# Six more Strassen-like groups in a one-core decoder layer, and a second place for the sums of w_up's activations

## The chip, the core and the metric

The kernel runs on one core of one Trainium2 chip, in float32. The metric is the device time of one execution in microseconds (us); before the change three runs took 1473.76, 1474.32 and 1475.28 us, a median of 1474.32. The profile is of one execution, whose span (first to last instruction) is 1471.1 us.

TensorE (PE) multiplies, with PEld as its weight load; VectorE (DVE) does elementwise work; ScalarE (ACT) does activations and copies; GpSimd (POOL) does next to nothing here; SyncE (SP) issues the DMA of the weights.

## The reference

One decoder layer on 256 tokens with a width of 2048:

```python
u = rmsnorm(h, norm_mix_pre)
P = u @ w_in                               # SSD z, x, B, C, dt and attention q, k, v
y_mix = concat(ssd(P), attention(P))       # 256 x 4096
h = h + rmsnorm(y_mix @ w_out, norm_mix_post)
u = rmsnorm(h, norm_mlp_pre)
hdn = relu(u @ w_up)                       # 256 x 8192
h = h + rmsnorm((hdn * hdn) @ w_down, norm_mlp_post)
```

What the change touches are the products with `w_out` (4096 x 2048), `w_up` (2048 x 8192) and `w_down` (8192 x 2048).

## The kernel before

**Three products for one.** Every float32 operand is split in a high part (`hi`, a rounded copy by ScalarE, L139) and a low part (`lo`, the rest, a subtraction by VectorE, L140). A product is then three matmuls: high by high, high by low and low by high (L262 to L264, or L344 to L346). A weight tile `raw` of 2 x 128 rows and 512 columns is loaded by SyncE (L149), split, and its parts stand in `hi` and `lo`, with five buffers each (`BUFS`, L44). `raw` has four buffers, and two more in the place of `uc` while the activations of the first stage are not needed (`fetch_next`, L190).

**Ordinary groups and sevens.** A unit (`unit`, L362) computes 1024 columns of the output, two blocks of 512, for all 256 tokens (two tiles of 128). It goes through groups `k` of 256 rows. An ordinary group makes 2 x 2 x 2 block products, 8, that is 24 matmuls, from two weight tiles. A seven (`seven`, L311) makes the same with 7 block products, 21 matmuls, in the manner of Strassen and Winograd: it needs sums of the weight blocks (four additions of 512 columns on VectorE, into `e`, into `t4` and in place into `raw_b`, L320 to L325) and four split tiles in place of two (`hl_a`, `hl_e` and `hl_b` of 1024 columns, `hl_t` of 512). It also needs sums of the activation blocks (`sums_of_acts`, L293), which are made once for each `k` and kept in the memory that `room["sums"]` lists, two entries for each `k`. Four more accumulators in PSUM (`more`) are folded into the result after the last seven of a unit (`combine_new`, L348; `combine_onto`, L893).

**Which group is a seven** is written by hand at each unit: `order_of(ks, by_seven)` gives the order of the groups and the set of sevens, and then follow the closing sets, which are always ordinary and go block by block: both tokens of the first 512 columns, then of the second.

**What sets the order of the work.** The Tile framework schedules instructions by priority. Loading, adding and splitting weights have a high priority (`AHEAD`), and are chained in the order in which the code writes them (`line`, `in_line`, L209 to L225): a group's additions and splits come before the next group's on VectorE and ScalarE. The sums of the activations of the next group, if it is a seven, are asked for before the present group (L369).

**The stages.** w_out's first five groups (L1080) run while the last attention heads finish, whose products stand between the matmuls; then the attention's memory is closed and the pool `hp` opened in its place (L1085 to L1087), which holds `e`, the temporaries `r`, the residual `h` and the mixing result `mw`. w_out's first unit goes on with groups 5 to 13 and the closing sets 14 and 15 (L1118). Its second unit (L1144) ends in `mix_to_up` (L916), an order written out by hand, which finishes the mixing result, adds it to `h` and starts `w_up`; it uses the memory of `ua`, in which sums of the second unit stand, for four weight parts. Then `h` goes out to DRAM (`out_of_place`, L1194), and its memory serves the sums of the `w_up` units: `ha` has six entries, which is three sums (`UP_SEVENS`, L52, is groups 2, 4 and 5). The first half of `w_up` has three units (L1240, `fb` 2, 4 and 6), each with groups 0 to 5 and the closing sets 6 and 7; `up_end` and `turned` (L1205, L1216) square, turn and split the result. The two units of the first half of `w_down` (L1245, L1247), the four of the second half of `w_up` and the two of the second half of `w_down` (L1265, L1270) follow. In the second unit of the latter, group 9 is a seven already; in w_out's second unit groups 8 and 10 are.

Of the kernel before, what the change touches and what calls it, by code (L numbers as in the profile page):

```python
# [10 lines left out]
F32 = mybir.dt.float32  # L11
F32R = mybir.dt.float32r
# [4 lines left out]
P = 128  # L17
S = 256
D = 2048
NT = S // P  # L20
# [19 lines left out]
KB = 2  # L40
# [11 lines left out]
UP_SEVENS = (2, 4, 5)  # L52
# [22 lines left out]
def hymba_layer(ctx: ExitStack, tc: tile.TileContext, x, norm_mix_pre, w_in, conv_w, conv_b, dt_bias, a_log,  # L75
# [3 lines left out]
    w_in, w_out, w_up, w_down = w_in[0], w_out[0], w_up[0], w_down[0]  # L79
# [44 lines left out]
    def bank():  # L124
        return pacc.tile([P, NB], F32, name="acc")

    def psmall():
        return psm.tile([P, NB], F32, name="ps")
# [7 lines left out]
    def split(hi, lo, src, scale=None):  # L136

        if scale is None:
            return (nc.scalar.activation(hi, src, AF.Copy),  # L139
                    nc.vector.tensor_tensor(lo, src, hi.bitcast(F32), op=ALU.subtract))  # L140
        return (nc.scalar.activation(hi, src, AF.Copy, scale=scale),  # L141
                nc.vector.scalar_tensor_tensor(lo, src, scale, hi.bitcast(F32), op0=ALU.mult, op1=ALU.subtract))
# [10 lines left out]
    def tmp():  # L153
        if "own" in room:
            room["own"].rotate(1)
            return room["own"][0]
        return hp.tile([P, NB], F32, name="r", bufs=2)
# [6 lines left out]
    room = {}  # L164
# [6 lines left out]
        room["acts"] = part  # L171
        sums_of.clear()

    def in_place_of_h(acts):

        a = hp.tile([P, 3 * KB, 2, S], F32R, name="ha")
        room["sums"] = [a[:, k] for k in range(3 * KB)]
        if acts is part:
            b = hp.tile([P, KB, 2, S], F32R, name="hb")
            room["sums"] += [b[:, k] for k in range(KB)]  # L180
            room["sums"] += [hp.tile([P, 2, S], F32R, name="wpost", bufs=2) for _ in range(2)]
        else:
            b = hp.tile([P, NT, NB], F32, name="hb")
            room["shared"] = [[b[:, t] for t in range(NT)],
                              [hp.tile([P, NB], F32, name="wpost", bufs=2) for _ in range(NT)]]
        room["raw"] = None
        room["acts"] = acts
        sums_of.clear()
# [22 lines left out]
    @contextmanager  # L211
    def in_line():

        with ExitStack() as order:
            for last in line.values():
                order.enter_context(tc.issue_after(last.ins))
            yield

    def split_in_line(hi, lo, raw):
        with in_line():  # L220
            line["act"], line["dve"] = split(hi, lo, raw)

    def add_in_line(dst, a, b):
        with in_line():
            line["dve"] = nc.vector.tensor_tensor(dst, a, b, op=ALU.add)  # L225
# [26 lines left out]
    def drain():  # L252
        while waiting:
            pump()
# [11 lines left out]
    def row_tiles(src, c0, ks, acc, acts, first=True, last=True, lag=0, at_end=None, pumps=1, fetch=fetch):  # L266


        held = {}
        n = len(ks)  # L270
        for i in range(n + lag):
            if i < n:
                held[i] = weights(src, ks[i] * KB, c0, fetch)
            for t, at in ((0, i), (1, i - lag)):
                if not 0 <= at < n:
                    continue
                row_tile(acc[t], t, held[at], ks[at], acts, first and at == 0, last and at == n - 1)
                if at == n - 1 and at_end:
                    at_end(t, acc[t])
            pump(pumps)  # L280
# [12 lines left out]
    def sums_of_acts(k):  # L293

        if k in sums_of:
            return sums_of[k]
        places = room["sums"][2 * len(sums_of):][:2]
        h_, l_, r = room["acts"](k * KB)
        with tc.high_priority(offset=AHEAD):
            a, c = (tmp().rearrange("p (i s) -> p i s", s=P) for _ in range(2))  # L300
            ah_, al_ = (v[:, r:r + KB].bitcast(F32).rearrange("p j (t s) -> p j t s", t=NT) for v in (h_, l_))
            nc.vector.tensor_tensor(a.rearrange("p (j t) s -> p j t s", t=NT), ah_, al_, op=ALU.add)
            nc.vector.tensor_tensor(c[:, 0:2], a[:, 0::3], a[:, 1:2].to_broadcast([P, 2, P]), op=ALU.subtract)
            nc.vector.tensor_tensor(c[:, 2], a[:, 0], c[:, 1], op=ALU.add)
            nc.vector.tensor_tensor(c[:, 3], a[:, 2], c[:, 2], op=ALU.subtract)
            ch, cl = (v.rearrange("p b (t s) -> p (b t) s", t=NT) for v in places)
            split(ch, cl, c)
        sums_of[k] = ch, cl
        return ch, cl
# [38 lines left out]
    def combine_new(dst, more):  # L348

        with tc.high_priority(offset=AHEAD):  # L350
            a, b = dst
            u = tmp()
            nc.scalar.activation(a[0], more[0], AF.Copy)
            nc.vector.tensor_tensor(u, a[0], more[2], op=ALU.subtract)
            nc.vector.tensor_tensor(a[1], more[3], u, op=ALU.add)
            nc.vector.tensor_tensor(b[0], more[1], u, op=ALU.add)
            nc.vector.tensor_tensor(b[1], more[3], b[0], op=ALU.add)

    def order_of(ks, by_seven):
        return [(k, k in by_seven) for k in ks]  # L360

    def unit(src, n, order, last, acc, more, combine, lag=0, at_end=(None, None), first=True, ending=None):  # L362


        cols = (n * NB, (n + 1) * NB)
        sevens = [k for k, by_seven in order if by_seven]
        for i, (k, by_seven) in enumerate(order):
            if i + 1 < len(order) and order[i + 1][1]:
                sums_of_acts(order[i + 1][0])  # L369
            if by_seven:  # L370
                if k == sevens[0]:
                    drain()
                seven(src, *cols, k, acc, more, k == sevens[0], k == sevens[-1])
            else:
                for b in range(2):
                    row_tiles(src, cols[b], [k], acc[b::2], room["acts"], first and i == 0, False,
                              fetch=fetch_next)
            if k == sevens[-1]:
                combine(more)
        for b in range(2):  # L380
            if b and ending:
                ended.append(ending(cols[b], last, acc))
            else:
                row_tiles(src, cols[b], last, acc[b::2], room["acts"], False, True, lag if b else 0, at_end[b],
                          fetch=fetch if b else fetch_next)
# [692 lines left out]
    acc = [bank() for _ in range(2 * NT)]  # L1078
    early = 5
# [7 lines left out]
    hp = ctx.enter_context(tc.tile_pool(name="hp", bufs=1, reuse_waits="tile"))  # L1087
# [11 lines left out]
    mw = hp.tile([P, NT, D], F32, name="mw")  # L1099
# [10 lines left out]
    more = [psmall(), bank(), psmall(), bank()]  # L1110

    def whole(n):
        def at_end(t, a):
# [1 line left out]
                mixed(n, t, a)  # L1115
        return at_end

    unit(w_out, 0, order_of(range(early, 14), (6, 9, 12)), (14, 15), acc, more,  # L1118
         lambda x: combine_new(in_mw(0), x), 0, (whole(0), whole(1)), first=False)
    for n in (2, 3):  # L1120
        load_wpost(norm_mix_post, n)
    acc, more = more, acc
# [71 lines left out]
    def out_of_place():  # L1194

        yield from copies(in_dram, of_h, 4)
        in_place_of_h(act_u)
        for k in UP_SEVENS:
            sums_of_acts(k)
            yield  # L1200

    def in_dram(t, cs):
        return h_d[:, t, cs]
# [24 lines left out]
    acc = gemm_features(w_up, NB, begun)  # L1228
# [6 lines left out]
    acc, more = [bank() for _ in range(2 * NT)], [psmall(), bank(), psmall(), bank()]  # L1235
    for hf in range(2):
        if hf:
            in_place_of_h(act_u)
        for fb in range(0 if hf else 2, 8, 2):
            unit(w_up[:, hf * 4096:], fb, order_of(range(6), UP_SEVENS), (6, 7), acc, more,  # L1240
                 lambda x: combine_new(room["shared"], x), 0, (up_end(fb, 0), up_end(fb + 1, 1)))
            acc, more = more, acc
        if hf == 0:
            in_place_of_h(part)
            unit(w_down, 0, order_of(range(14), (4, 6, 9, 11, 13)), (14, 15), acc, more,  # L1245
                 lambda x: combine_new(in_mw(0), x), 0, (onto(0), onto(1)))
            unit(w_down, 2, order_of((0, 1, 4, 2, 6, 3, 9, 5, 11, 7, 13, 8), (4, 6, 9, 11, 13)), (10, 12, 14, 15), more, acc,  # L1247
                 lambda x: combine_new(in_mw(2), x), 0, (onto(2), onto(3)))
# [13 lines left out]
    in_place_of_u()  # L1262
    for n in range(2):
        load_wpost(norm_mlp_post, n)
    unit(w_down[4096:], 0, order_of(range(14), (3, 6, 8, 11, 13)), (14, 15), acc, more,  # L1265
         lambda x: combine_onto(0, x), 0, (complete(0), complete(1)))
    for n in (2, 3):
        load_wpost(norm_mlp_post, n)
# [26 lines left out]
```

## Time and profile before

| | before |
|---|---|
| median of three runs | 1474.32 us |
| span of the profiled execution | 1471.1 us |
| what lies around the span (median less span) | 3.2 us |
| mean granted TensorE clock | 0.998 |
| weights and parameters read from HBM | 281.78 MB |

The profile's page gives the busy time of each engine, the chain of waits that ended last, and the costliest groups of instructions. A stretch row gives, for a piece of the span, the busy time of each engine with its number of instructions. A timeline row gives the start, the duration, the engine, the line, what is written and what is read, and in square brackets the idle time before it with what ended it. Matmuls are pipelined: each is shown as longer than its distance to the next, so that TensorE's busy time is not a sum of durations.

### The profile page before, as it was taken

To read this page: it belongs to the slowest core of one execution; us is meant where nothing else is said; L and a number is where in the kernel's file an instruction comes from. 1 tells how busy PE (TensorE), PEld (TensorE's weight loads), DVE (VectorE), ACT (ScalarE), POOL (GpSimd) and SP (SyncE) were. 2 spreads that over 40 slices of the span, in tenths; PEclk is the share of its full clock that TensorE was granted. 3 is DMA by queue.
4 is the path that set the end of the run, shared out by engine and by line. 5 is a ranking of instruction groups with operands and counts; after the bars stand their busy time and mean duration, and the time that the engine had idled before them with its cause. 6 is when DMAs were issued, how large, how long until landed. Compare 5 with 4: busy or idle time off the path is not lost.

```text
span 1471.1 us, 20006 instructions
## 1 busy us (share of the span) xinstructions
PE 1461.2 (99%) x7216; PEld 1231.4 (84%) x7216; DVE 1239.6 (84%) x1849; ACT 861.1 (59%) x1188; POOL 47.8 (3%) x67
## 2 busy tenths in 40 slices
PE   9999999999999999999999999999999999999998
PEld 8888888888888888888888888888888888888886
DVE  6798797898497696588989989889887898989998
ACT  7475675465456565555557566655554666665553
POOL 0003100210000000000000000000000000000000
PEclk9999999999999999999999999999999999999999
DMA  7665566555657476566657566655665666576853
GB/s 272 208 205 182 179 184 194 174 172 167 177 168 207 122 208 192 191 229 210 204 177 237 165 194 201 210 175 191 213 223 174 201 201 205 172 235 202 273 200 114
DMA packets 151299, 287.31 MB, mean 195 GB/s; under 512 B 11696, under 2 KB 14624, under 8 KB 151200
## 3 DMA queue, kind: packets, MB, share of 16 engines
q1 hardware_dynamic: 143472, 272.50, 58.9%
q10 hardware_dynamic: 7728, 13.54, 2.8%
q8 instruction: 56, 0.92, 0.3%
q14 instruction: 43, 0.35, 0.1%
HBM read 281.78 MB, written 4.23 MB: 194 GB/s over the span
## 4 chain that ended last, share of the span: by engine, by line
PE 94%; DVE 3%; issue 1%; ACT 1%; DMA 1%; POOL 0%; POOLq 0%; SPq 0%; ACTq 0%; DVEq 0%
PE acc L393 17%; PE acc L262 12%; PE acc L263 12%; PE acc L264 12%; PE acc L396 9%; PE acc L345 4%; PE acc L346 4%; PE acc L344 4%; PE ps L263 3%; PE ps L262 3%; PE ps L264 3%; PE ps L346 2%; PE ps L344 2%; PE ps L345 2%; DVE lo L140 1%
## 5 line engine op out<-in xcount | busy, mean ns | idle before, releaser
L139 ACT ACTIVATE hi<-raw 128x1024 fp32r<-128x1024 f32 (+1 forms) x477 | 499.0, 1053 | 387.9 <-PE acc L393 111.9
L140 DVE TENSOR_TENSOR lo<-raw,hi 128x1024 fp32r<-128x1024 f32 (+1 forms) x477 | 579.9, 1220 | 135.7 <-ACT hi L139 127.9
L393 PE MATMUL acc<-ua,hi 128*128 128x512 f32 x680 | 186.3, 402 | 0.0
L393 PEld LDWEIGHTS acc<-ua,hi 128*128 128x128 f32 x680 | 119.7, 189 | 18.7
L262 PE MATMUL acc<-hi,ua 128*128 128x512 f32 x280 | 112.0, 400 | 0.0
L396 PEld LDWEIGHTS acc<-ua,lo 128*128 128x128 f32 x680 | 99.8, 189 | 11.6
L264 PE MATMUL acc<-hi,ua 128*128 128x512 f32 x280 | 109.3, 391 | 0.0
L263 PE MATMUL acc<-lo,ua 128*128 128x512 f32 x280 | 109.3, 390 | 0.0
L396 PE MATMUL acc<-ua,lo 128*128 128x256 f32 x680 | 102.9, 281 | 0.0
L262 PE MATMUL acc<-hi,sh 128*128 128x512 f32 x224 | 88.7, 397 | 0.0
L264 PE MATMUL acc<-hi,sl 128*128 128x512 f32 x224 | 87.3, 390 | 0.0
L263 PE MATMUL acc<-lo,sh 128*128 128x512 f32 x224 | 87.3, 390 | 0.0
L139 ACT ACTIVATE hi<-e 128x1024 fp32r<-128x1024 f32 x51 | 54.1, 1062 | 55.5 <-DVE e L225 50.3
L393 PE MATMUL acc<-uc,hi 128*128 128x512 f32 x272 | 77.6, 398 | 0.0
L263 PE MATMUL acc<-lo,ah 128*128 128x512 f32 x168 | 65.5, 390 | 0.4 <-DVE lo L140 0.4
L264 PE MATMUL acc<-hi,al 128*128 128x512 f32 x168 | 65.4, 389 | 0.0
L262 PE MATMUL acc<-hi,ah 128*128 128x512 f32 x168 | 65.4, 389 | 0.0
L264 PEld LDWEIGHTS acc<-hi,ua 128*128 128x128 f32 x280 | 52.6, 188 | 11.6
L140 DVE TENSOR_TENSOR lo<-e,hi 128x1024 fp32r<-128x1024 f32 x51 | 62.0, 1216 | 0.0
L262 PEld LDWEIGHTS acc<-hi,ua 128*128 128x128 f32 x280 | 52.6, 188 | 10.4 <-ACT ua L141 0.3
L263 PEld LDWEIGHTS acc<-lo,ua 128*128 128x128 f32 x280 | 52.7, 188 | 10.0
L264 PE MATMUL acc<-hi,uc 128*128 128x512 f32 x144 | 56.0, 389 | 0.0
(475 smaller groups left out, 3060.9 us busy)
## 6 DMA issues: line engine op xcount, KB each, us to landing
raw<-in_w_in_dram SPq DMA_DIRECT2D x189, 512.0 KB, 3.6
raw<-in_w_up_dram SPq DMA_DIRECT2D x128, 512.0 KB, 3.9
raw<-in_w_down_dram SPq DMA_DIRECT2D x110, 512.0 KB, 4.7
raw<-in_w_out_dram SPq DMA_DIRECT2D x46, 512.0 KB, 4.2
uc<-in_w_out_dram SPq DMA_DIRECT2D x18, 512.0 KB, 4.5
uc<-in_w_down_dram SPq DMA_DIRECT2D x18, 512.0 KB, 5.1
bc<-acs_d ACTq DMA_DIRECT2D x8, 512.0 KB, 4.5
xs<-in_x_dram SPq DMA_DIRECT2D x8, 256.0 KB, 6.3
```

Of the source, the lines that this page charges most:

```text
L139: return (nc.scalar.activation(hi, src, AF.Copy), nc.vector.tensor_tensor(lo, src, hi.bitcast(F32), op=ALU.subtract))
L140: nc.vector.tensor_tensor(lo, src, hi.bitcast(F32), op=ALU.subtract))
L262: nc.tensor.matmul(dst, a_h[:, r, ts], hi[:, j], start=begin and j == 0, stop=False)
L263: nc.tensor.matmul(dst, a_h[:, r, ts], lo[:, j], start=False, stop=False)
L264: product[t] = nc.tensor.matmul(dst, a_l[:, r, ts], hi[:, j], start=False, stop=end and j == KB - 1)
L344: nc.tensor.matmul(dst, a_h, hi[:, j], start=own and first, stop=False)
L345: nc.tensor.matmul(dst, a_h, lo[:, j], start=False, stop=False)
L346: nc.tensor.matmul(dst, a_l, hi[:, j], start=False, stop=own and last)
L393: nc.tensor.matmul(acc[f], hi[:, j, f * P:(f + 1) * P], u(k0 + j), start=k0 + j == 0, stop=False, skip_group_check=True)
L396: nc.tensor.matmul(acc[f][:, 0], lo[:, j, f * P:(f + 1) * P], u(k0 + j)[:, 0], start=False, stop=k0 + j == NK - 1, skip_group_check=True)
```

## The change

Four units get other orders or sets of sevens, six groups in all become sevens, and w_up's sums get memory for a fourth group:

```diff
-    def in_place_of_h(acts):
+    def in_place_of_h(acts, hf=0):
         a = hp.tile([P, 3 * KB, 2, S], F32R, name="ha")
         room["sums"] = [a[:, k] for k in range(3 * KB)]
+        if acts is not part and not hf:
+            c = hp.tile([P, 4 * KB, 2, S], F32R, name="mw")
+            room["sums"] += [c[:, k] for k in range(4 * KB)]
...
-    unit(w_out, 0, order_of(range(early, 14), (6, 9, 12)), (14, 15), acc, more,
+    unit(w_out, 0, order_of((6, 5, 8, 7, 9, 11, 10, 13, 12), (6, 8, 9, 10, 12)), (14, 15), acc, more,
...
         for k in UP_SEVENS:
             sums_of_acts(k)
             yield
+        sums_of_acts(1)
...
-            in_place_of_h(act_u)
+            in_place_of_h(act_u, hf)
         for fb in range(0 if hf else 2, 8, 2):
-            unit(w_up[:, hf * 4096:], fb, order_of(range(6), UP_SEVENS), (6, 7), acc, more,
+            unit(w_up[:, hf * 4096:], fb, order_of(range(6), UP_SEVENS if hf else (1,) + UP_SEVENS), (6, 7), acc, more,
...
             in_place_of_h(part)
+            mw = hp.tile([P, NT, D], F32, name="mw")
...
-    unit(w_down[4096:], 0, order_of(range(14), (3, 6, 8, 11, 13)), (14, 15), acc, more,
+    unit(w_down[4096:], 0, order_of((0, 1, 2, 3, 4, 6, 5, 8, 7, 9, 10, 11, 12, 13), (3, 6, 8, 9, 11, 13)), (14, 15), acc, more,
```

- **w_out, first unit:** groups 8 and 10 become sevens beside 6, 9 and 12, and the order alternates: 6, 5, 8, 7, 9, 11, 10, 13, 12, with a seven first and last. The sums of 8 and 10, which the second unit makes before, are made here.
- **w_up, first half, three units:** group 1 becomes a seven beside 2, 4 and 5; the order stays 0 to 5. Its sums stand in the memory of `mw`, which is given back before w_down's first unit writes its result there.
- **w_down, second half, first unit:** group 9 becomes a seven, and from group 6 on ordinary groups and sevens alternate. The sum of 9 is made here and not in the second unit.

The number of weight loads and their sizes are the same.

## The prediction

> **What bounds the kernel now.** I read the page first, for the engine that sets the end, and then the busy time of each engine over the stretches that the change touches.
>
> ```profile
> span 1471.1 us, 20006 instructions
> PE 1461.2 (99%) x7216; PEld 1231.4 (84%) x7216; DVE 1239.6 (84%) x1849; ACT 861.1 (59%) x1188; POOL 47.8 (3%) x67
> PE 94%; DVE 3%; issue 1%; ACT 1%; DMA 1%; POOL 0%; POOLq 0%; SPq 0%; ACTq 0%; DVEq 0%
> ```
>
> TensorE sets the time: 94% of the chain of waits is its own work. VectorE is busy for 84% of the span as a mean, but a mean says nothing of the stages in question. In the next table each row is a stretch: w_out's first unit and its second, a stretch with a TensorE gap, the three w_up units of the first half, and the first unit of w_down's second half.
>
> ```profile
> core 0: us, PE busy (x) PEld busy (x) DVE busy (x) ACT busy (x) POOL busy (x), PEclk, DMA share, GB/s
> 630.45:688.36 57.91, 57.91 (x258) 47.95 (x257) 51.86 (x68) 32.58 (x39) 0.00 (x0) 1.00 0.74 248
> 688.36:760.80 72.44, 72.44 (x321) 60.00 (x320) 68.29 (x87) 42.92 (x50) 0.00 (x0) 1.00 0.60 200
> 764.00:774.00 10.00, 9.06 (x44) 7.03 (x43) 6.74 (x10) 4.23 (x9) 1.49 (x1) 1.00 0.41 127
> 822.69:864.64 41.95, 41.95 (x190) 34.74 (x189) 36.98 (x46) 26.57 (x32) 0.00 (x0) 1.00 0.62 186
> 864.64:908.11 43.47, 43.47 (x202) 35.93 (x201) 38.66 (x46) 28.17 (x36) 0.00 (x0) 1.00 0.64 195
> 908.11:951.40 43.29, 43.29 (x200) 35.74 (x199) 38.66 (x46) 28.63 (x36) 0.00 (x0) 1.00 0.62 191
> 1292.90:1377.40 84.50, 84.50 (x382) 69.95 (x381) 78.36 (x102) 49.31 (x58) 0.00 (x0) 1.00 0.67 218
> ```
>
> In all six unit rows TensorE is busy to the last 0.01 us, so a product left out there is time left out, as long as VectorE keeps up. But VectorE has only 6.05 us free in w_out's first unit (57.91 - 51.86), 4.81 in a steady w_up unit (43.47 - 38.66) and 6.14 in the w_down unit. ScalarE has over 15 us free in each and decides nothing.
>
> **What one more seven-product group saves and costs.** w_out's first unit holds six ordinary groups and two closing sets of 24 matmuls and three groups of 21: 255 in 57.91 us, 0.227 us each. A group made a seven leaves out three: 0.68 us. Six of them: 4.1 us of TensorE.
>
> For VectorE's price I read the first seven of that unit, in order of time:
>
> ```profile
> 628.09 0.68 DVE L302 TENSOR_TENSOR r<-sh,sl 128x512 f32<-128x512 f32 x1
> 630.74 0.69 DVE L225 TENSOR_TENSOR e<-raw 128x512 f32<-128x512 f32 x1 [1.96 <-PE ps L794]
> 631.34 0.42 DVE L303 TENSOR_TENSOR r<-r 128x256 f32<-128x256 f32 x1
> 631.68 0.68 DVE L225 TENSOR_TENSOR e<-e,raw 128x512 f32<-128x512 f32 x1
> 632.28 0.28 DVE L304 TENSOR_TENSOR r<-r 128x128 f32<-128x128 f32 x1
> 632.48 1.22 DVE L140 TENSOR_TENSOR lo<-raw,hi 128x1024 fp32r<-128x1024 f32 x1
> 633.62 0.28 DVE L305 TENSOR_TENSOR r<-r 128x128 f32<-128x128 f32 x1
> 633.82 0.42 DVE L140 TENSOR_TENSOR al<-ps,ah 128x256 fp32r<-128x256 f32 x1
> 634.15 0.68 DVE L225 TENSOR_TENSOR r<-e,raw 128x512 f32<-128x512 f32 x1
> 634.75 0.68 DVE L225 TENSOR_TENSOR raw<-raw 128x512 f32<-128x512 f32 x1
> 635.36 0.68 DVE L140 TENSOR_TENSOR ua<-r,ua 128x512 fp32r<-128x512 f32 x1
> 636.07 0.69 DVE L302 TENSOR_TENSOR r<-ah,al 128x512 f32<-128x512 f32 x1
> 636.68 1.22 DVE L140 TENSOR_TENSOR lo<-e,hi 128x1024 fp32r<-128x1024 f32 x1
> 637.82 1.22 DVE L140 TENSOR_TENSOR lo<-raw,hi 128x1024 fp32r<-128x1024 f32 x1
> 638.95 0.68 DVE L140 TENSOR_TENSOR lo<-r,hi 128x512 fp32r<-128x512 f32 x1
> 639.55 2.35 DVE L140 TENSOR_TENSOR lo<-uc,hi 128x1024 fp32r<-128x1024 f32 x2
> 641.83 0.42 DVE L303 TENSOR_TENSOR r<-r 128x256 f32<-128x256 f32 x1
> ```
>
> I count from start to start, since each begins some 0.08 us before the end shown for the last: 0.60 for 512 columns, 1.135 for 1024, 0.34 for 256, 0.20 for 128. An ordinary group is two low parts: 2.28 us (639.55 to 641.83). A seven is four additions (L225), three low parts of 1024 and one of 512: 4 x 0.60 + 3 x 1.135 + 0.60 = 6.43. The sums of the activations (L302 to L305 and their low part) are 0.60 + 0.34 + 0.20 + 0.20 + 0.60 = 1.95, paid once for each place. So a conversion adds 4.15 us to VectorE and takes 0.68 from TensorE. On its own a seven asks 6.43 of VectorE against 21 x 0.227 = 4.77 of TensorE. Beside an ordinary group, the pair asks 8.7 against 10.2 and fits; with the sums in it, it asks 10.66 against 10.22 and does not.
>
> [...]
>
> **w_out's first unit (two conversions, two more sums).** Here the new order begins with a seven, where the old one began with ordinary group 5. The rows above say when a seven can begin: its first addition waited until 630.74 for the last attention product (L794), since the tile `e` lies in a pool that opens only then. TensorE came to the unit at 630.45:
>
> ```profile
> 630.31 0.38 PE L794 MATMUL ps<-pT,tk 128*128 128x128 f32 x2
> 630.45 0.47 PE L262 MATMUL acc<-hi,sh 128*128 128x512 f32 x1
> 636.00 0.39 PE L344 MATMUL ps<-hi,sh 128*128 128x512 f32 x1
> 640.54 0.39 PE L345 MATMUL acc<-lo,sh 128*128 128x512 f32 x1
> ```
>
> Before, group 5, whose low parts were ready early, covered 630.45 to 636.00, and the seven's last low part (638.95) came 0.9 us ahead of its product (640.54). Now nothing covers it, and the additions and splits are chained in the written order, so group 5's cannot slip ahead. From 630.74 VectorE has, up to the last seven (12): five sevens 32.15, ordinary groups 5, 7, 11, 13 at 2.28 = 9.1, five sums 9.75 less the L302 already done 0.6, and the attention's `al` 0.34: 50.7 us, to 681.5. Its alternating pairs are just the 10.66 ones, so TensorE never gets ahead again. It ends group 12 some 0.5 us later, at 682.0, and then has four closing sets of 2.72 us, 10.9, to 692.9, for which VectorE needs only 4 x 1.135 and the combination. Before, this was 688.36. Cost: **+4.6 us**, of which nearly 5 is the opening gap and the rest the pairs, less the 1.4 saved. Bounds: -1.4 if all is hidden, +8 if two thirds of VectorE's 6 us of pauses in that row come back on top.
>
> The second unit gets these two sums for nothing: VectorE 68.29 - 3.9 against 72.44 of TensorE, so the backlog is worked off there; 0. `mix_to_up` writes into `ua`, which is now read until group 10's seven and not 8's; its first write into it follows two weight tiles that take their place from sets after group 10. No new wait; 0.
>
> **w_up's first half (three conversions).** TensorE 43.47 - 0.68 = 42.79; VectorE 38.66 + 4.15 = 42.81. There is no reserve left, and two places have sevens in a row (1, 2 and 4, 5). What VectorE still idles becomes TensorE's wait. Its pauses in such a unit, and what they hang on:
>
> ```profile
> 861.69 1.23 DVE L140 TENSOR_TENSOR lo<-raw,hi 128x1024 fp32r<-128x1024 f32 x1 [0.31 <-ACT hi L139]
> 864.91 1.23 DVE L140 TENSOR_TENSOR lo<-raw,hi 128x1024 fp32r<-128x1024 f32 x1 [1.99 <-ACT hi L139]
> 878.35 2.59 DVE L140 TENSOR_TENSOR lo<-raw,hi 128x1024 fp32r<-128x1024 f32 x2 [1.96 <-ACT hi L139]
> ```
>
> ```profile
> DVE lo L140 <- ACT hi L139: 138.5, 137, 2.5
> ACT hi L139 <- DMA raw<-in_w_up_dram: 23.9, 23, 1.6
> ```
>
> The two long ones are full buffers (the high part waits for TensorE to free one of five); they go when VectorE is late. What stays is 0.5 us of small ones (4.81 - 0.31 - 1.99 - 1.96) and about one weight load per unit, 23.9/23 = 1.0 us. I take 1.5: a unit then lasts 42.81 + 1.5 = 44.3, +0.85. The first unit starts with VectorE well ahead (41.95 - 36.98 = 5 us free), so it gains its 0.68. Together **+1.0 us**. Bounds: -2.0 (nothing stays) and 3 x 4.16 = +12.5 (all of it stays). I stay near the low end, as the long pauses are buffers. The sum for place 1 is made before these units, from 0 to 1.95 us, taken as 0 in that lead; its memory, `mw`, is read last before the w_up units begin.
>
> **w_down's second half (one conversion, one sum moved forward).** VectorE 78.36 + 4.15 + 1.95 = 84.5 against 84.50 - 0.68 = 83.8. That is over by 0.6, but three ordinary groups come first and the closing sets last, and the next unit loses the sum; low parts made ahead carry it. **-0.7**, bounds -0.7 and +2.
>
> **Sum.** 4.6 + 1.0 - 0.7 = +4.9. The span 1471.1 becomes 1476.0; the median of the runs, 1474.32, has 3.2 us around the span, so 1479.2 us.
>
> **The rivals.** *All hidden:* the products left out come out whole, 1474.3 - 4.1 = 1470.2, faster. For it: not a wait in TensorE's rows, where VectorE already is at 90%. Against: the opening seven. It decides if the first seven's low parts are there by 635. Chance 0.12. *Only the opening costs:* w_up's buffers absorb its conversions, 4.6 - 2.0 - 0.7 = +1.9, 1476.2; it needs VectorE free of pauses, 0.20. *w_up falls behind:* weight loads and sevens in a row keep 3.5 us of pause in all three units, 3 x 2.84 = 8.5, so 4.6 + 8.5 - 0.7 = +12.4, 1486.7; 0.18. *The clock drops:* TensorE stands for most of 3 us at 630.45, and should it then run a group at half speed, 4.8 us are added at the most, some 2.4 in the middle, 1481.6; the 764 row shows 1.00 granted through 0.94 us of gap, which is shorter; 0.05. [...]
>
> **How the numbers follow.** The forecast has 0.45, the rivals 0.12, 0.20, 0.18, 0.05. A measurement tells 0.2% (2.9 us) from no change. Faster is the hidden case, 0.12; same is the third case, 0.20; slower the other three, 0.68. The range 1472 to 1486 leaves out the hidden case and the top of the w_up case, under 2 in 10.
>
> **What would show it.** After 630 the first seven-product matmul (L344) should be followed by waits on low parts (L140), TensorE's sevens there should each stand behind theirs, and the row of w_out's first unit should last about 62.5 us. The second and third w_up unit should take 44.3, with VectorE over 95% busy; the w_down unit 83.8. I am wrong if L344's group 6 runs through without gap, or if w_up's units last 42.8.

## The result, and the profile after

| | before | after |
|---|---|---|
| median of four runs each, taken side by side | 1474.80 us | 1492.47 us (1489.26 to 1494.33) |
| ratio, 95% interval | | 1.0122 (1.0106 to 1.0138) |
| span of the profiled execution | 1471.1 us | 1492.5 us |
| mean granted TensorE clock | 0.998 | 0.996 |

The change makes the kernel slower by 18 us. The forecast was 1479.2 us with a range of 1472 to 1486: right in direction, and 13 us too low.

The page of after begins with the span and the busy time of each engine, and in its chain of waits TensorE's own work has fallen from 94% to 82%, with 10% for VectorE and 4% for transfers:

```profile
span 1492.5 us, 20018 instructions
PE 1468.5 (98%) x7198; PEld 1229.1 (82%) x7198; DVE 1266.0 (85%) x1890; ACT 867.2 (58%) x1201; POOL 47.8 (3%) x67
PE 82%; DVE 10%; DMA 4%; issue 2%; ACT 2%; POOL 0%; ACTq 0%; POOLq 0%; SPq 0%; DVEq 0%
```

The stretches of after, in the columns shown before: w_out's first unit, the three w_up units of the first half, and the first unit of w_down's second half:

```profile
632.18:697.12 64.94, 60.98 (x252) 48.26 (x251) 62.78 (x88) 37.32 (x45) 0.00 (x0) 0.95 0.67 219
831.50:878.14 46.64, 42.46 (x183) 33.39 (x181) 42.69 (x56) 28.46 (x37) 0.00 (x0) 1.00 0.56 162
878.14:924.82 46.68, 43.96 (x198) 35.09 (x196) 43.05 (x53) 29.58 (x37) 0.00 (x0) 1.00 0.61 180
924.82:970.99 46.17, 44.09 (x197) 34.93 (x196) 43.20 (x53) 29.56 (x37) 0.00 (x0) 1.00 0.59 181
1312.74:1397.00 84.26, 84.10 (x376) 68.59 (x375) 80.75 (x111) 49.70 (x60) 0.00 (x0) 1.00 0.63 210
```

Against 57.91, 41.95, 43.47, 43.29 and 84.50 before, w_out's unit costs 7.0 us, the w_up units 4.7, 3.2 and 2.9 (10.8 in all), and the w_down unit gives back 0.2, but what follows it, up to the end of the span, is 1.8 us longer (95.5 for 93.7): 1.6 together. What lies between these stretches is the same to 0.3 us. The profiled run also came 1.7 us later to w_out's unit (632.18 for 630.45), a difference ahead of the change, and was 1.9 us over the median.

**w_out.** The opening of after's first unit, in order of time:

```profile
632.19 0.47 PE L348 MATMUL ps<-hi,sh 128*128 128x512 f32 x1
632.47 0.69 DVE L229 TENSOR_TENSOR e<-raw 128x512 f32<-128x512 f32 x1 [1.96 <-PE ps L798]
634.22 1.22 DVE L140 TENSOR_TENSOR lo<-raw,hi 128x1024 fp32r<-128x1024 f32 x1
635.49 0.50 PE L349 MATMUL ps<-lo,sh 128*128 128x512 f32 x1 [2.60 <-DVE lo L140]
639.69 0.80 PE L349 MATMUL acc<-lo,ua 128*128 128x512 f32 x1 [0.58 <-DVE lo L140]
641.14 0.63 PE L350 MATMUL ps<-hi,ua 128*128 128x512 f32 x1
641.56 0.63 PE L349 MATMUL acc<-lo,ua 128*128 128x512 f32 x1
644.64 0.39 PE L266 MATMUL acc<-hi,sh 128*128 128x512 f32 x1
```

The seven begins as forecast. TensorE does its first high products and stands 2.60 us for the first low part, and the products behind follow VectorE's parts one by one. At 641.14 matmuls start 0.42 us apart and not 0.23: the clock has halved (granted clock 0.50 and 0.53 in the rows of the last section). The first seven ends at 644.64, after 12.5 us instead of 4.8.

**w_up.** What VectorE waited for in the three units (total, times, longest in us), and the piece of the chain of waits about the second unit's second load wait (start, duration, what):

```profile
DVE e L229 <- DMA raw<-in_w_up_dram: 6.2, 5, 2.0
DVE lo L140 <- ACT hi L139: 2.0, 5, 0.6
```

```profile
892.73 1.07 ACT hi L139
893.82 1.24 DVE lo L140
895.07 3.62 DMA raw<-in_w_up_dram
898.82 0.70 DVE e L229
```

VectorE's low part ends at 895.06, that frees a buffer of `raw`, the load into it lands 3.62 us later, and only then can the next seven's first addition begin. Before, VectorE met no load wait of its own in these units; all that is listed for it there is

```profile
DVE lo L140 <- ACT hi L139: 11.0, 7, 2.5
```

TensorE, which had no listed wait there before, now waits mostly for high parts of ScalarE. That does not make ScalarE the cause (it is busy for 28 to 30 us of a unit): in the run with w_up changed alone, ScalarE's high parts wait longest for VectorE's additions. The first row is TensorE's in after, the second ScalarE's in that run:

```profile
PE acc L348 <- ACT hi L139: 8.1, 11, 1.2
ACT hi L139 <- DVE e L229: 20.9, 9, 3.4
```

### The profile page after: what moved, and what is told of

It reads as the page before. It is cut to its first block, busy times and chain, and to the rows that moved or that the text cites. A ratio compares the mean times of both kernels' runs of the same rounds, so it can differ in the third digit from the quotient of the medians.

```text
span 1492.5 us, 20018 instructions
## 1 busy us (share of the span) xinstructions
PE 1468.5 (98%) x7198; PEld 1229.1 (82%) x7198; DVE 1266.0 (85%) x1890; ACT 867.2 (58%) x1201; POOL 47.8 (3%) x67
## 4 chain that ended last, share of the span: by engine, by line
PE 82%; DVE 10%; DMA 4%; issue 2%; ACT 2%; POOL 0%; ACTq 0%; POOLq 0%; SPq 0%; DVEq 0%
PE acc L397 16%; PE acc L266 10%; PE acc L267 10%; PE acc L268 10%; PE acc L400 8%; DVE lo L140 4%; PE acc L349 4%; PE acc L350 4%; PE acc L348 4%; PE ps L267 2%; PE ps L266 2%; PE ps L268 2%; DMA raw<-in_w_up_dram 2%; DVE e L229 2%; DMA raw<-in_w_down_dram 2%
## 5 line engine op out<-in xcount | busy, mean ns | idle before, releaser
L266 PE MATMUL acc<-hi,ua 128*128 128x512 f32 x260 | 103.9, 400 | 0.0
L139 ACT ACTIVATE hi<-e 128x1024 fp32r<-128x1024 f32 x57 | 60.5, 1062 | 73.3 <-DVE e L229 64.5
L267 PE MATMUL acc<-lo,ua 128*128 128x512 f32 x260 | 101.5, 391 | 0.0
L268 PE MATMUL acc<-hi,ua 128*128 128x512 f32 x260 | 101.5, 390 | 0.0
L140 DVE TENSOR_TENSOR lo<-e,hi 128x1024 fp32r<-128x1024 f32 x57 | 69.3, 1216 | 0.7 <-ACT hi L139 0.7
L268 PEld LDWEIGHTS acc<-hi,ua 128*128 128x128 f32 x260 | 48.8, 188 | 10.7
L268 PE MATMUL acc<-hi,al 128*128 128x512 f32 x148 | 57.6, 389 | 0.0
L267 PE MATMUL acc<-lo,ah 128*128 128x512 f32 x148 | 57.6, 389 | 0.0
L266 PE MATMUL acc<-hi,ah 128*128 128x512 f32 x148 | 57.2, 390 | 0.0
L266 PEld LDWEIGHTS acc<-hi,ua 128*128 128x128 f32 x260 | 48.8, 188 | 9.7 <-ACT ua L141 0.3
L267 PEld LDWEIGHTS acc<-lo,ua 128*128 128x128 f32 x260 | 48.9, 188 | 9.3
```

Source lines behind the costliest of these rows:

```text
L139: return (nc.scalar.activation(hi, src, AF.Copy), nc.vector.tensor_tensor(lo, src, hi.bitcast(F32), op=ALU.subtract))
L266: nc.tensor.matmul(dst, a_h[:, r, ts], hi[:, j], start=begin and j == 0, stop=False)
L267: nc.tensor.matmul(dst, a_h[:, r, ts], lo[:, j], start=False, stop=False)
L268: product[t] = nc.tensor.matmul(dst, a_l[:, r, ts], hi[:, j], start=False, stop=end and j == KB - 1)
```

## The experiments

Ratios are against runs of the kernel before on the same chip (medians 1473.05 for the first four, 1473.42 for the next four, 1473.09 and 1473.40 for the last two pairs).

**One part at a time.** Each of the three places alone, the other two as before.

```diff
+    unit(w_out, 0, order_of((6, 5, 8, 7, 9, 11, 10, 13, 12), (6, 8, 9, 10, 12)), ...   # first run
+    order_of(range(6), UP_SEVENS if hf else (1,) + UP_SEVENS), ...                     # second run
+    unit(w_down[4096:], 0, order_of((0, 1, 2, 3, 4, 6, 5, 8, 7, 9, 10, ...             # third run
```

> The kernel before with w_out's new order and two more sevens alone. Theory (the parts add up; the unit loses at its opening): the unit from its first matmul to the next unit's takes 64.9 us as in the changed kernel (57.9 before), the execution about +7 us. If the clock stays at 1.00 in the opening, +4.3. Rival (VectorE paces all alternating pairs): gaps ahead of every seven, not at the first alone, some 0.5 us each.

> w_up's three conversions alone, with the sums in the mixing result's memory. Theory (VectorE has no reserve, and waits for weight loads): the three units take 46.6, 46.7 and 46.2 us in place of 43.5, VectorE is busy over 92% there, and the execution is +11 us. Rival (VectorE enters w_up late only because of w_out's backlog in the changed kernel): the first unit stays at 43 and the sum is under +5.

> w_down's one conversion alone. Theory: as in the changed kernel, +0.25 us in the first unit and +1.06 in the second, +1.3 together, within noise. Rival (the loss there is a shift of that one execution): -0.7.

Measured: w_out alone 1479.41 us, ratio 1.0044 (1.0029 to 1.0059); w_up alone 1484.35, 1.0076 (1.0061 to 1.0091); w_down alone 1474.97, 1.0011 (1.0002 to 1.0020). That is 6.4, 11.3 and 1.9 us, 19.6 together, against some 18 for the whole: the parts add up within the noise, and w_up is the largest. In that run the first w_up unit lasts 46.40 us by itself, so its loss is not a backlog from w_out. The first unit of w_out with its own change alone, and the first of w_down, then the first seven of w_down's second unit:

```profile
630.16:694.08 63.92, 60.66 (x253) 46.52 (x251) 62.81 (x88) 36.78 (x45) 0.00 (x0) 0.97 0.67 223
```

```profile
1294.00:1378.48 84.48, 84.33 (x376) 68.41 (x375) 80.70 (x111) 49.96 (x60) 0.00 (x0) 1.00 0.61 210
```

```profile
1393.49 0.47 PE L344 MATMUL acc<-hi,ua 128*128 128x512 f32 x1 [0.96 <-DVE mw L1254]
```

In w_out TensorE's long waits stand at the first seven alone; by the starts of its matmuls, a product of the later ones is at most 0.25 us late. w_down's unit comes out at 84.5, no shorter than before for its three missing matmuls, and at the first seven of the next unit TensorE stands 0.96 us for VectorE, which is still busy with the first unit's ending (L1254). From the unit's start to the end of the span this run takes 179.8 us for 178.2 before: a loss of 1.6, not the gain of 0.7.

**The opening by itself.** Only groups 5 and 6 change places; sevens 6, 9, 12 as before, so no work is added.

```diff
-    unit(w_out, 0, order_of(range(early, 14), (6, 9, 12)), (14, 15), acc, more,
+    unit(w_out, 0, order_of((6, 5, 7, 8, 9, 10, 11, 12, 13), (6, 9, 12)), (14, 15), acc, more,
```

> The kernel before with groups 5 and 6 of w_out's first unit exchanged, so that it begins with a seven; no product, sum or load is added or left out. Theory (the loss of w_out is the opening): the first seven takes over 9 us in place of 4.8, with its low parts last to come, and the unit is 5 us longer, up to 8 if the clock drops to half in the gap. Rival (it is the two added sevens): under +1 us.

Then the same with 24 small matmuls of ones ahead of the first seven, so that TensorE doesn't stand there.

```diff
                 if k == sevens[0]:
                     drain()
+                    for _ in range(fill):
+                        nc.tensor.matmul(more[1][:, 0:P], ones, ones, start=True, stop=True)
```

> The exchanged groups 6 and 5 again, with 24 matmuls of ones (128 columns, their result is overwritten) ahead of the first seven, so that TensorE works through the gap of 630 to 635. Theory (a part of the opening's price is the clock, which falls to half after the gap): the clock stays at 1.00 over the unit, which then lasts 57.9 plus the wait for the low parts alone, about 62 us in place of 63.6. Rival (the clock costs nothing, since TensorE waits for the low parts in that stretch anyway): 63.6 as without the filling.

Measured: 1479.62, 1.0044 (1.0027 to 1.0061), and 1478.66, 1.0032 (1.0020 to 1.0044). The unit and the stretch of the low clock of the first, and the unit of the second with the filling matmuls' row:

```profile
630.78:694.42 63.64, 60.46 (x258) 48.37 (x257) 55.03 (x70) 34.88 (x41) 0.00 (x0) 0.97 0.72 242
634.02:637.43 3.41, 3.35 (x7) 1.89 (x7) 3.38 (x8) 3.17 (x5) 0.00 (x0) 0.52 0.98 345
```

```profile
630.53:693.80 63.27, 63.27 (x307) 53.32 (x305) 54.60 (x70) 34.20 (x41) 0.00 (x0) 1.00 0.71 243
```

```profile
630.61 5.52 PE L375 MATMUL acc<-ones 128*128 128x128 f32 x48
```

The exchange alone costs 5.7 us of the unit (63.64 for 57.91), nearly all of what w_out's whole change costs. With the filling the clock never falls, and yet the unit lasts 63.27; the 62 us that the theory gave are missed by 1.3. But the 0.4 us between the two is not the price of the clock. The filling lasts longer than the gap: the seven's first product starts only at 635.89, and from there on no product waits, so in this run TensorE, with 5.5 us of unwanted work, sets the end. A full row of TensorE proves nothing if what fills it is not wanted. The run without filling says more of the clock:

```profile
638.28 0.51 PE L345 MATMUL acc<-lo,ua 128*128 128x512 f32 x1 [0.58 <-DVE lo L140]
```

Behind its stretch at half clock TensorE stands another 0.58 us for the second low part, until 7.50 us after the unit's start. In after, where the clock falls 5.2 us into the unit and not 3.4, the same wait ends 7.51 us after the start (639.69). So the low clock of this run only filled time in which TensorE would have waited for VectorE.

**More loads in flight for w_up.** The sums of group 1 go to the attention's memory, and the memory of `mw` holds further `raw` buffers, so that six loads can be under way.

```diff
-            c = hp.tile([P, 4 * KB, 2, S], F32R, name="mw")
-            room["sums"] += [c[:, k] for k in range(4 * KB)]
+            room["sums"] += [v[:, NK - KB:] for v in (ah, al)]
+            extra = hp.tile([P, NT, D], F32, name="mw").rearrange("p t (k n) -> p (t k) n", n=NB)
...
-        room["raw"] = None
+        room["raw"] = extra if acts is not part and not hf else None
```

> w_up's three conversions alone, as before, with six weight loads in flight in place of four: two more buffers lie in the mixing result's memory, and the sums of group 1 lie in the memory of the attention's output. Theory (VectorE's pauses there are the wait for weight loads, 3 to 4 us in each unit): VectorE is busy to over 98%, the units last 43.5 (the first up to 45), and the execution is +1 to +3 us in place of +11. Rival (VectorE's own work, or the order of TensorE's products, sets the units): over 45.5 each, +9 or more.

Measured: 1480.47, 1.0047 (1.0033 to 1.0061). Both numbers that were expected miss; it lies half way. The three units and VectorE's load waits in them, first of w_up alone with four buffers, then with six loads (the sum row is of the three units: length, then busy time of each engine):

```profile
sum 138.92, PE 130.74 PEld 103.51 DVE 128.98 ACT 87.96 POOL 0.00; mean PE 43.58 PEld 34.50 DVE 42.99 ACT 29.32 POOL 0.00
```

```profile
DVE e L229 <- DMA raw<-in_w_up_dram: 5.8, 5, 1.6
```

```profile
sum 134.97, PE 129.39 PEld 103.58 DVE 128.92 ACT 87.53 POOL 0.00; mean PE 43.13 PEld 34.53 DVE 42.97 ACT 29.18 POOL 0.00
```

```profile
DVE e L230 <- DMA raw<-in_w_up_dram: 1.9, 1, 1.9
```

VectorE's work is the same, its load waits fall by 3.9 us, and the units by 3.95. That leaves 6.3 us over the 128.71 of before. (The sums of group 1 also lie elsewhere in this run; that this changes nothing was not tried by itself.)

**Other orders in w_out.** An ordinary group stays first; one group more becomes a seven, and then two.

```diff
+    unit(w_out, 0, order_of((5, 6, 7, 8, 10, 9, 11, 12, 13), (6, 8, 9, 12)), ...       # one more
+    unit(w_out, 0, order_of((5, 6, 7, 8, 11, 9, 13, 10, 12), (6, 8, 9, 10, 12)), ...   # two more
```

> The kernel before with one more seven in w_out's first unit (group 8) and an ordinary group first: 5, 6, 7, 8, 10, 9, 11, 12, 13. VectorE has 6.05 us free there and gets 6.1 more. Theory (a seven more pays where its work on VectorE finds room and its low parts are made under an ordinary group): no gap at the opening, the unit 57.2 in place of 57.9, -0.7 us. Rival (the sum and the seven in that unit cost more than the products saved): 58.5 or more.

> Both more sevens of w_out's first unit as in the changed kernel, but with an ordinary group first and the two last sevens in a row: 5, 6, 7, 8, 11, 9, 13, 10, 12. VectorE has 6.05 us free and gets 12.2. Theory (past the free time VectorE paces): no gap at the opening, gaps of 3 to 4 us together at the last sevens, the unit near 60.5. Rival (only the opening costs): 56.6.

Measured: 1473.69, 1.0001 (0.9992 to 1.0010), and 1477.65, 1.0029 (1.0018 to 1.0040). The units:

```profile
630.28:688.84 58.56, 58.36 (x256) 47.08 (x254) 54.85 (x76) 32.72 (x40) 0.00 (x0) 1.00 0.71 235
```

```profile
631.04:693.31 62.27, 59.34 (x253) 47.58 (x251) 60.91 (x86) 34.93 (x43) 0.00 (x0) 0.97 0.64 213
```

One conversion behind an ordinary opening gains nothing, and two cost 4.4 us: VectorE, busy for 60.91 us, no longer fits under the unit of 57.91. So the opening's 5.7 us and these 4.4 do not add up to the whole change's 6.0. VectorE is busy there for 62.81 of 63.92 us: TensorE's late start and VectorE's added work fall into the same time. The first lies at the rival's 58.5, the second over the 60.5 that was expected; one period at half clock is in it (last section).

**VectorE's work in w_up.** One of the seven's four additions goes to GpSimd, with six loads in flight and with four.

```diff
             add_in_line(e[:, 0], raw_a[:, 0], raw_b[:, 0])
+            nc.gpsimd.tensor_tensor(raw_b[:, 0], raw_b[:, 0], raw_b[:, 1], op=ALU.add)
             add_in_line(e[:, 1], e[:, 0], raw_b[:, 1])
...
-            add_in_line(raw_b[:, 0], raw_b[:, 0], raw_b[:, 1])
```

> w_up's first half as in the run with six loads in flight, and the addition within raw_b (one 512-column addition of the four of a seven) goes from VectorE to GpSimd in the units' four sevens. Output unchanged. Four times 0.60 us are 2.4 us less of VectorE in a unit, 41.3 of some 43.6 instead of 43.0 to 43.7. Theory (with loads in flight, what is left of the cost is VectorE's own work): the units fall from 45.0 as a mean to 43.2 to 43.7, the sum over three units to +1.0 or less against before (128.6), the whole to some 1473 to 1475 us. First rival (TensorE's fixed order where two sevens stand in a row, each behind its own chain of addition, high part and low part): the chain is as long, the units stay at 44.5 or more, some 1478 us. Second rival (GpSimd is slow at it: 0.72 us for 256 columns in the trace, so 1.4 for 512, and the high part behind it comes later): units of 46 or more.

> w_up's three conversions alone with four buffers of raw weights, as in the change, and the addition within raw_b on GpSimd in the units' four sevens. Output unchanged. If the late loads are only a consequence of VectorE's being late (a buffer comes free when VectorE has read it), 2.4 us less work per unit takes the waits away too: units of 43.2 to 43.7, some 1473 to 1475 us. If four buffers are too few for two sevens in a row whatever VectorE does, the waits for loads stay, units of 44.5 to 45.5, some 1479 to 1481 us.

Measured: 1485.55, 1.0085 (1.0070 to 1.0100), and 1487.35, 1.0098 (1.0081 to 1.0115): both slower than with the addition on VectorE. The units of each, and one such addition beside VectorE's low part, from the first:

```profile
sum 140.32, PE 131.81 PEld 104.54 DVE 133.79 ACT 89.49 POOL 18.93; mean PE 43.94 PEld 34.85 DVE 44.60 ACT 29.83 POOL 6.31
```

```profile
888.84 1.21 DVE L140 TENSOR_TENSOR lo<-mw,hi 128x1024 fp32r<-128x1024 f32 x1
...
890.78 1.74 POOL L329 TENSOR_TENSOR raw<-raw 128x512 f32<-128x512 f32 x1 [7.56 <-DVE e L232]
891.29 2.33 DVE L140 TENSOR_TENSOR lo<-raw,hi 128x1024 fp32r<-128x1024 f32 x1
```

```profile
sum 141.60, PE 132.38 PEld 104.40 DVE 131.76 ACT 89.24 POOL 18.43; mean PE 44.13 PEld 34.80 DVE 43.92 ACT 29.75 POOL 6.14
```

The units, 46.8 us each as a mean in the first run, are in the second rival's range, but its reason, a slow GpSimd, is not what the rows show. VectorE is held up meanwhile: the low part begun at 891.29 lasts 2.33 us instead of 1.21. Eleven of GpSimd's additions fall in these units; if each holds VectorE up by 1.1 us, an estimate, that is some 12 us in all. VectorE's busy time shows as much: it rises by 4.87 us where 7.2 were to go, and the units by 5.35, with one period at half clock in the first of them (a granted mean of 0.96). How much of the remaining 0.5 us is GpSimd's slowness (1.74 us for an addition that takes VectorE 0.68) was not tried. So the trial did not take VectorE's work away; it added to it, and the time followed.

**The same work left out.** The addition is dropped in the sevens of these units, so the work really goes (what the sevens compute is then not the layer's).

```diff
-            add_in_line(raw_b[:, 0], raw_b[:, 0], raw_b[:, 1])
+            if not room["less"]:
+                add_in_line(raw_b[:, 0], raw_b[:, 0], raw_b[:, 1])
```

> w_up's three conversions alone with four buffers of raw weights, as in the change, and the addition within raw_b left out in all sevens of the units of w_up's first half (the output is then not the reference's): four times 0.60 us less of VectorE per unit, 2.4 us, with the same loads, splits and products. If the cost lies in VectorE's work and the late loads only follow from it, the units fall from 46.3 to 43.0 to 43.8, the whole to some 1474 to 1476 us. If four buffers of raw weights are the cause by themselves, the waits for loads stay as long and the units stay at 45 or more, some 1481 us.

> The same addition left out, with six loads in flight (the output is not the reference's). If the two causes add up, the units fall by the same from 45.0, to 43 or less, near TensorE's own 42.8: some 1473 to 1474 us. If TensorE's fixed order of sevens in a row holds the rest, the units stay at 44 or more and the run at 1477 us or more.

Measured: 1476.45, 1.0022 (1.0013 to 1.0031), and 1473.89, 1.0004 (0.9995 to 1.0013). The units with four buffers, then with six loads:

```profile
sum 130.71, PE 128.76 PEld 103.86 DVE 120.74 ACT 87.12 POOL 0.00; mean PE 42.92 PEld 34.62 DVE 40.25 ACT 29.04 POOL 0.00
```

```profile
DVE e L231 <- DMA raw<-in_w_up_dram: 5.0, 5, 1.1
```

```profile
sum 128.96, PE 127.45 PEld 104.23 DVE 121.06 ACT 87.47 POOL 0.00; mean PE 42.48 PEld 34.74 DVE 40.35 ACT 29.16 POOL 0.00
```

```profile
866.90:909.74 42.84, 42.84 (x198) 35.32 (x197) 39.40 (x48) 28.77 (x37) 0.00 (x0) 1.00 0.67 203
```

Put side by side, the sums of the three units (before: 128.71 us, VectorE busy 114.30):

| w_up's conversions | units, us | VectorE busy | its load waits |
|---|---|---|---|
| four buffers | 138.92 | 128.98 | 5.8 |
| six loads in flight | 134.97 | 128.92 | 1.9 |
| four buffers, one addition on GpSimd | 141.60 | 131.76 | 5.3 |
| six loads, one addition on GpSimd | 140.32 | 133.79 | 0.8 |
| four buffers, one addition left out | 130.71 | 120.74 | 5.0 |
| six loads, one addition left out | 128.96 | 121.06 | 1.1 |

With four buffers and one addition less, VectorE's busy time falls by 8.24 us (7.2 were expected) and the units by 8.21. The time is what the theory of this run gave, but the load waits, which by it should have gone too, stay at 5.0: the late loads do not only follow from VectorE's lateness. Work and load waits both count, nearly in full, as long as VectorE is the longer line. In the last row it no longer is: there the load waits fall by 3.9 us and the units only by 1.75, and the middle unit runs at 42.84 us with TensorE full, so that TensorE sets the pace again. Even then the whole is 1473.89 us, no faster than before. No version in these runs beats the kernel before.

## Why the prediction was wrong

**What failed: the pauses in w_up, "I take 1.5", and the first w_up unit, which "gains its 0.68".** VectorE's work was forecast at 42.81 us for a unit; with w_up changed alone it is 42.52, 43.04 and 43.42, a mean of 42.99. The rest of the unit was to be 1.5 us; it is 3.3 (138.92 - 128.98 = 9.94, over three). Of the 9.2 us by which w_up is over its forecast of +1.0 in this run, the first unit has 5.1 (46.40 - 41.95 = 4.45 lost, 0.68 to be gained), the other two 4.1. Two steps of the working led there.

- *"About one weight load per unit, 1.0 us"* was read from ScalarE's waits of before, when VectorE had slack. In after VectorE's additions themselves wait for loads, 6.2 us in five waits. There are four buffers, and the next tile lies in one only 3.6 to 4.8 us after VectorE has let it go. Three of the five (0.9 to 1.1 us) stand at group 4, whose second tile takes the place of group 2's; the two longest (2.0 and 1.3) stand at group 1, whose tile takes the place of one of the closing sets before. Six loads in flight took 3.95 us off the three units, so this is some 4 of the 10.
- *"The first unit starts with VectorE well ahead (5 us free)."* Those 5 us were pauses within the unit (41.95 - 36.98 = 4.97), and the unit asked for more than them: VectorE's busy time there went from 36.98 to 42.69, 5.7 more. That is the conversion (4.15) and 1.6 us more. The prediction took the sum for group 1 as 0, since it would be made before these units; in after most of it lies in the first one, from 831.74 to its low part, four operations of 1.6 us from start to start:

```profile
831.74 0.43 DVE L307 TENSOR_TENSOR r<-r 128x256 f32<-128x256 f32 x1
834.13 0.69 DVE L140 TENSOR_TENSOR mw<-r,mw 128x512 fp32r<-128x512 f32 x1
```

The rest, some 6 us, is VectorE's line being longer than TensorE's once its pauses stay. In units with 43.0 us of work against 42.8 of TensorE, the pauses of VectorE become time. The third rival, "w_up falls behind", had just this: 3.5 us of pause in every unit, +8.5. In after the pauses are 3.5 (139.49 - 128.93, over three); the first unit's loss makes it 10.8. It was given a chance of 0.18, since the long pauses of before were full buffers. They did go, as the prediction said (11.0 us of waits for high parts before, 2.0 after); load waits took their place. One reading of the working was off by little: the pause of 0.31 us at 861.69 lies in the unit before the one that it is taken from; that unit's own third pause is 0.50, at 905.35.

**w_out: the right mechanism, a size too small.** The cost came as the working had it: VectorE's line paces the unit from its first addition on. With w_out changed alone, VectorE works from 630.44 to 681.87, the last low part of the last seven, with one pause of 0.6 us: 51.4 us for the 50.7 of the sum. TensorE's closing sets begin 1.0 us behind it, at 682.90, and not 0.5, and take 11.2 us and not 10.9. These three make the +4.6 into +6.0. "Of which nearly 5 is the opening gap" held in kind: the exchange of two groups alone costs 5.7. In after's profile w_out cost 7.0, and there the clock was low for two periods (last section). The unit was to last 62.5 us and lasted 63.9 alone, 64.9 in after.

**w_down: the wrong sign.** "Low parts made ahead carry it", -0.7, was wrong: the unit gained nothing alone (84.48), and the backlog of VectorE met the next unit's first seven (0.96 us). By the profiles it is +1.6, in after and alone, within the bound of +2 that the prediction gave.

**What held.** The unit rows with TensorE busy to the last 0.01 us did not mean that a product left out is time left out; the prediction's condition, "as long as VectorE keeps up", was the whole question. The price of a conversion by starts, 4.15 us, gave the mean work of a w_up unit within 0.2 us, but that mean has the first unit in it, which had less to do before (36.98 us); the second and third, with 43.04 and 43.42 (43.05 and 43.20 in after), are 0.2 to 0.6 over. The rival of the clock was given 0.05, with 2.4 us for a group at half speed. The clock did fall to half (granted 0.50 in after, from 637.40 to 644.23); at the opening it cost nothing where one period was low, and about 1 us where two were.

The range ended at 1486, since it left out just the cases in which all of the pauses stay (up to +12.5 for w_up, which was listed as a bound). With that bound in it, it would have reached 1490.7, still 1.8 short.

## What to carry to other kernels

When work moves from a full engine to one that then has as much to do, do not price the second engine at its work alone: here its pauses stayed, 3.3 us of a w_up unit, and counted nearly in full. Ask of each pause whether its cause goes when that engine runs late: here the waits for high parts, the long ones behind full buffers, fell from 11.0 us to 2.0, and waits for loads that start only when this engine frees their place came, 6.2 us. A stage should not open with the group whose preparation is longest: here the exchange of two groups, with no work added, cost 5.7 us. Another opening does not save a stage whose second engine has too much to do: behind an ordinary group the two conversions still cost 4.4 us.

## What the hardware showed that was not expected

**The clock changed on a grid of 3.41 us, and a half-idle period was enough.** Five stretches of after about the opening, one period each, and then three periods of the run with two more sevens in w_out:

```profile
630.76:634.18 3.42, 2.13 (x11) 1.50 (x9) 1.71 (x4) 0.38 (x1) 0.00 (x0) 1.00 0.12 35
634.18:637.59 3.41, 1.48 (x5) 0.96 (x6) 3.41 (x7) 1.92 (x3) 0.00 (x0) 0.97 0.94 290
637.59:641.00 3.41, 2.83 (x6) 1.56 (x6) 3.38 (x5) 3.09 (x4) 0.00 (x0) 0.50 1.00 390
641.00:644.42 3.42, 3.42 (x10) 2.64 (x10) 3.42 (x6) 1.06 (x1) 0.00 (x0) 0.53 0.91 326
644.42:647.83 3.41, 3.41 (x17) 2.82 (x16) 3.41 (x6) 1.70 (x2) 0.00 (x0) 1.00 0.82 291
```

```profile
669.04:672.45 3.41, 1.56 (x7) 0.88 (x6) 3.39 (x5) 2.56 (x4) 0.00 (x0) 1.00 0.39 130
672.45:675.86 3.41, 3.41 (x9) 2.65 (x8) 3.38 (x5) 1.19 (x2) 0.00 (x0) 0.50 0.45 159
675.86:679.28 3.42, 2.50 (x11) 1.69 (x9) 2.77 (x4) 2.03 (x4) 0.00 (x0) 1.00 0.36 126
```

A period in which TensorE was busy for 1.48 or 1.56 us of 3.41 was followed by one at half clock; periods of 2.13 and 2.50 us were not. (The rows of after are not quite on the grid: the 0.97 shows that the clock fell 0.2 us ahead of that row's end, at 637.40. From 633.99 to there TensorE was busy for 1.29 us. The clock rose at 644.23, two periods later, and fell again at 1487.32, after 247 more.) In after, 2.83 us of work at half clock were followed by a second half period; in the run with only the opening exchanged, 3.35 us were followed by full clock. The same gap of 2.60 us at the opening thus led to one half period in two runs and to two in another. Where it was one, it cost nothing, since TensorE had to wait for the same low part anyway. Where it was two, the first seven ended 12.5 us after its start and not 10.6 (641.38 - 630.78 in the run with the exchange alone), and the unit was 1.0 us longer than the same unit with one (64.94 for 63.92).

**VectorE was held up while GpSimd added.** With six loads in flight and one addition on GpSimd, the low part from 891.29 lasts 2.33 us: GpSimd's addition ends at 892.52, and an undisturbed low part of 1.21 us from there ends at 893.73, near its 893.62. The next row of this kind is alike: beside the addition from 897.83 to 899.57 the low part from 898.34 lasts 2.32 us. To move 0.60 us of work to an engine that stood idle cost VectorE 1.1 there.
